# Branch A's norm factors: written to memory and read back into all partitions, instead of transposed by TensorE

## The chip, the core and the metric

The kernel runs on one core of one Trainium2 chip. The metric is the device time of one execution in microseconds (us). The core has five engines that run side by side, each through its own queue in order: TensorE (PE in the profile, with its weight loads as PEld), VectorE (DVE), ScalarE (ACT), GpSimd (POOL) and SyncE (SP), which here issues nearly all DMAs. TensorE writes to PSUM, which has eight banks of 128 x 512 float32. DVE and ACT read PSUM; POOL and the DMAs work on SBUF and on memory.

## What is computed

The program is one encoder block on 1024 tokens (and 16 meta tokens) of width 1024, all in float32. Cut to what matters here:

```
h = x + mixer(rms_norm(x));  h = h + swiglu(rms_norm(h));  out = rms_norm(h)

mixer:  y_a = differential_attention(q, k, v)       # branch A: 4 heads, v of width 128, all keys
        y_b = windowed_gqa(q, k, v, sink)           # branch B: 8 heads, window 128
        merged = sigmoid(ga) * (y_a @ w_ba) + sigmoid(gb) * (y_b @ w_bb)
        return merged @ w_o

differential_attention, at its end, for each token and head:
        y = y * rsqrt(mean(y * y over the 128 values) + 1e-6) * subln_gain * (1 - lambda_init)
```

The change is in that last line: one factor per token and head, `rsqrt(mean(y*y) + eps)`, has to reach the 128 values of that token.

## The kernel before

**Stages.** First x is normed and transposed, the projections are made, and branch B's attention runs (to about 306 us in the profile). Branch A's q, k and v go to memory by head (`qa_d`, `ka_d`, `va_d`). Then comes branch A's attention, to about 621 us: four heads h, each over eight tiles t of 128 query tokens, with the projection of the gates (`pp_g`, line 201) laid between its steps as filler for TensorE. After it come the branch outputs and gates (`ppa`, line 552), the product with w_o, and the feed-forward block, whose products are split into seven half-sized ones.

**One tile of branch A.** `scores_a` (from line 595 on) makes the scores of two maps, m = 1 and then m = 0, each in three chunks of keys (line 608, 352, 352 and 336 columns). DVE takes each chunk out of PSUM, adds the distance term and keeps the running minimum (line 614); ACT takes the exponent (619), DVE the reciprocal of the sum (620); POOL scales one map (622) and DVE combines the two (625). One tile later `transpose_a` turns the result by TensorE (637), with ACT and DVE splitting it into a high and a low part (640, 641). `values_a` multiplies by v (650) in three parts, for two tiles together. Its result has the 128 values of the head in the partitions and the tokens along the row: `py`, 128 x 512 for four tiles.

**The norm.** After every fourth tile `normed_a` (from 654 on) works on such a 128 x 512 block, which is called a chunk here: eight in all, c = 0 and 1 for each head. ACT squares it into `ysq` and scales a copy `yg` by the gain. Four matmuls sum the squares over the partitions: `ysq`'s 128 columns are the stationary operand and a column of ones is the moving one (663), so that token 128 i + p has its sum in partition p, column i of `pst`. DVE takes the mean (665), and POOL raises it to the power -1/2 (666) into `f`, 128 x 4. Three steps later four transposes (671) of a column of `f`, repeated 128 times, put the factor of each token in all 128 partitions of the PSUM bank `pf`; DVE multiplies `yg` by it (672), and SP stores the block to `ya_d` (673).

**The order.** TensorE's order is written out by hand. For each tile the string `SLOTS` (`SLOTS_LAST` in the last head) names the steps: s is the next score chunk, g is one step of a gate projection (three matmuls of 512 columns), t a group of transposes, and n a step of the tail. The tail is a list of generators, `values_a` followed, after every fourth tile, by `normed_a`; each n runs the first generator to its next `yield`, and a `for` loop of `N_WAIT` = 3 yields keeps the transposes of `f` away from their sums. At the start of a head ten g steps run in one piece. The other engines' orders and SP's order of DMAs are made by a scheduler when the program is built. The scores, the transposes, `pst` and `pf` share five PSUM banks (tag "sc"); a sixth one waits for the first to be read. q and k have one buffer for each map, so that the next head's loads (584 to 587) wait for the last scores of this head.

The functions that the diff touches, and those that call them:

Of the kernel before, what the change touches and what calls it, by code (L numbers as in the profile page):

```python
# [9 lines left out]
F32 = mybir.dt.float32  # L10
# [4 lines left out]
ALU = mybir.AluOpType  # L15
# [4 lines left out]
P = 128  # L20
# [7 lines left out]
AH = 4  # L28
# [5 lines left out]
LAMBDA_INIT = 0.2  # L34
FAR = 1e32
SC = 5
N_WAIT = 3
PP2 = 2
COMBINE_POOL = (0, 1, 2, 3)
SLOTS = "sgsgsngsgsgstntnt"  # L40
# [31 lines left out]
def encoder_block(ctx: ExitStack, tc: tile.TileContext, x, meta, norm_mix, w_in, lq1, lk1, lq2, lk2,  # L72
                  subln, sink, w_ba, w_bb, w_o, norm_ffn, w_g, w_u, w_d, norm_final, out, dbg=None):
    nc = tc.nc
# [8 lines left out]
    def pool(name, side="left", space=None, bufs=1):  # L83
        kw = {} if space is None else {"space": space}
        if space is not DRAM:
            kw["reuse_waits"] = "tile"
        cm = tc.tile_pool(name=name, bufs=bufs, side=side, **kw)
        p = cm.__enter__()
        return p, lambda: cm.__exit__(None, None, None)
# [3 lines left out]
    dram, close_dram = pool("dram", space=DRAM)  # L93

    def bank(p, tag, name, bufs):
        return p.tile([P, 512], F32, tag=tag, name=name, bufs=bufs)
# [3 lines left out]
    va_d = [dram.tile([P, 2, 9, P], F32, name=f"va_d{h}") for h in range(AH)]  # L100
    g_d = [dram.tile([P, S], F32, name=f"g_d{i}") for i in range(16)]
    ya_d = [dram.tile([P, S], F32, name=f"ya_d{h}") for h in range(4)]
    yb_d = [dram.tile([P, S], F32, name=f"yb_d{h}") for h in range(4)]

    ident = const.tile([P, P], F32, name="ident")
    make_identity(nc, ident)
    ones = const.tile([P, 1], F32, name="ones")
# [45 lines left out]
    psum2 = None  # L153
# [416 lines left out]
    apool, close_apool = pool("apool")  # L570
    psum2, close_psum2 = pool("psum2", space=PSUM)
# [82 lines left out]
    def normed_a(h, c, py):  # L654
        nm = f"{h}_{c}"
        ysq = apool.tile([P, 512], F32, tag="ysq", name=f"ysq_{nm}", bufs=1)
        nc.scalar.activation(ysq, py, AF.Square)
        yg = apool.tile([P, 512], F32, tag="yg", name=f"yg_{nm}", bufs=2)
        nc.scalar.activation(yg, py, AF.Copy, scale=gsub)
        yield  # L660
        pst = bank(psum2, "sc", f"apst_{nm}", SC)
        for i in range(4):
            nc.tensor.matmul(pst[:, i:i + 1], ysq[:, i * P:(i + 1) * P], ones, start=True, stop=True)
        f = small.tile([P, 4], F32, tag="af", name=f"af_{nm}", bufs=2)
        nc.vector.tensor_scalar(f, pst[:, 0:4], 1.0 / P, EPS, ALU.mult, ALU.add)
        nc.gpsimd.tensor_tensor(f, f, neg_half, ALU.pow)
        for _ in range(N_WAIT):
            yield
        pf = bank(psum2, "sc", f"apf_{nm}", SC)
        for i in range(4):  # L670
            nc.tensor.transpose(pf[:, i * P:(i + 1) * P], f[:, i:i + 1].broadcast_to([P, P]), ident)
        nc.vector.tensor_tensor(yg, yg, pf, ALU.mult)
        nc.sync.dma_start(ya_d[h][:, c * 512:c * 512 + 512], yg)
        yield

# [16 lines left out]
    def later(done):  # L692
        h, t, s, at_, v = done
        if t % 4 == 1:
            acc[0] = bank(psum2, "acc", f"apy_{h}_{t}", 1)
        yield from values_a(h, t, v, at_, acc[0])
        if t % 4 == 3:
            yield from normed_a(h, t // 4, acc[0])
# [9 lines left out]
    for n in range(AH * NT + T_LAG):  # L708
        scoring, turning = iter(()), iter(())
        if n < AH * NT:  # L710
            h, t = divmod(n, NT)
# [661 lines left out]
    for n in range(nf, len(steps)):  # L1373
        p, j = steps[n][1]
# [6 lines left out]
        if p in LOADS:  # L1381
            at, half, col = LOADS[p]
            if at <= j < at + 4:
                t, cols = 4 * half + j - at, slice(col * 512, col * 512 + 512)
# [63 lines left out]
```

## Time and profile before

| | |
|---|---|
| three timed runs | 1450.67, 1455.43 and 1457.50 us; median 1455.43 us |
| the profiled execution | 1448.28 us, of which the span of the profile is 1446.4 us |
| TensorE matmuls | 1429.9 us busy, 99% of the span |
| TensorE weight loads | 1228.3 us, 85% |
| DVE, ACT, POOL | 893.4 us (62%), 676.4 us (47%), 462.3 us (32%) |
| granted TensorE clock, mean | 0.997 of full speed |
| memory | 129.14 MB read, 53.94 MB written |
| the 32 transposes of `f` | 272 ns each, from 383.3 to 621.7 us |
| the 64 weight loads of `ysq` | 192 ns each, from 376.0 to 614.9 us |

A row of the timeline has the start and the length in us, the engine, the line, the operation, what it writes <- what it reads, and how many stand together. Matmuls are pipelined: the next one starts before the last one's record ends, so that the cost of one is the distance between starts, not the length of the record. A matmul of two float32 operands that are not rounded has two weight loads and two matmuls in the trace; so the 32 sums appear 64 times.

### The profile page before, as it was taken

How to read it: one execution, taken by the hardware profiler on the slowest of the kernel's cores; microseconds unless marked ns; L12 is line 12 of the kernel's file. 1: busy time of each engine (PE TensorE's matmuls, PEld its weight loads, DVE VectorE, ACT ScalarE, POOL GpSimd, SP SyncE). 2: the span in 40 equal slices, each digit the busy share in tenths (PEclk: the TensorE clock that was granted, in tenths of full speed). 3: DMA queues.
4: the chain of work that ended last, by engine and by line, in shares of the span. 5: the costliest groups of instructions: out<-in, count | busy, mean ns of one | idle time of the engine just before them, and what ended most of it. 6: DMA issues, size and time to landing. Idle time of an engine off the chain costs nothing.

```text
span 1446.4 us, 20973 instructions
## 1 busy us (share of the span) xinstructions
PE 1429.9 (99%) x7327; PEld 1228.3 (85%) x7327; DVE 893.4 (62%) x1756; ACT 676.4 (47%) x1275; POOL 462.3 (32%) x454
## 2 busy tenths in 40 slices
PE   8999999999999999999999999999999999999998
PEld 7998989888898989888878778888888888888886
DVE  6456326528787868545787955654455543787566
ACT  6356436535554545555345844333333333444444
POOL 4143223323332222221513035454444442000442
PEclk9999999999999999999999999999999999999999
DMA  7334443363424242077341633433223322964343
GB/s 239 88 102 114 112 126 100 77 200 106 144 84 147 74 147 75 30 263 246 103 166 73 182 109 110 138 131 103 102 95 109 102 100 96 343 206 141 126 124 146
DMA packets 158617, 191.01 MB, mean 132 GB/s; under 512 B 16096, under 2 KB 103584, under 8 KB 158512
## 3 DMA queue, kind: packets, MB, share of 16 engines
q1 hardware_dynamic: 157936, 188.63, 40.8%
q8 instruction: 58, 0.95, 0.3%
q10 hardware_dynamic: 576, 1.05, 0.2%
q14 instruction: 47, 0.39, 0.1%
HBM read 129.14 MB, written 53.94 MB: 127 GB/s over the span
## 4 chain that ended last, share of the span: by engine, by line
PE 89%; DMA 4%; DVE 3%; ACT 1%; issue 1%; POOL 1%; SPq 0%; ACTq 0%; DVEq 0%
PE pg L1219 27%; PE pd L1315 14%; PE pp_g L201 12%; PE aps L608 4%; PE po L1122 4%; PE apy L650 3%; PE pp_va L201 3%; PE pp_ka L201 3%; PE pp_qb L201 3%; PE pp_qa L201 3%; PE apt L637 2%; PE bpt L339 2%; PE bpy L345 2%; PE po L1130 2%; PE bps L314 2%
## 5 line engine op out<-in xcount | busy, mean ns | idle before, releaser
L1219 PE MATMUL pg<-t,wop 128*128 128x512 f32 x1056 | 242.4, 389 | 0.0
L1219 PEld LDWEIGHTS pg<-t,wop 128*128 128x128 f32 x1056 | 198.2, 188 | 41.2
L1315 PE MATMUL pd<-ob,oa 128*128 128x512 f32 x924 | 209.6, 389 | 0.0
L1315 PEld LDWEIGHTS pd<-ob,oa 128*128 128x128 f32 x924 | 173.4, 188 | 36.0
L114 POOL TENSOR_TENSOR wop<-wf,wop 128x512 fp32r<-128x512 f32 x114 | 149.4, 1311 | 166.6 <-ACT wop L113 156.7
L1219 PE MATMUL pg<-b,wop 128*128 128x512 f32 x792 | 184.2, 390 | 2.1 <-DVE c L1236 1.9
L1219 PEld LDWEIGHTS pg<-b,wop 128*128 128x128 f32 x792 | 148.2, 188 | 34.2 <-DVE c L1236 2.8
L114 POOL TENSOR_TENSOR wl_c<-w_c,wh_c 128x1024 fp32r<-128x1024 f32 x32 | 77.6, 2426 | 162.1 <-ACT wh_c L113 142.5
L113 ACT ACTIVATE wop<-wf 128x512 fp32r<-128x512 f32 x128 | 80.8, 633 | 80.9 <-PE pg L1219 53.3
L619 ACT ACTIVATE as<-as,amn 128x1040 f32<-128x1040 f32 x64 | 74.5, 1164 | 73.8 <-DVE amn L614 73.6
L201 PE MATMUL pp_g<-hT_hi,wh_c 128*128 128x512 f32 x256 | 101.3, 396 | 0.0
L201 PE MATMUL pp_g<-hT_hi,wl_c 128*128 128x512 f32 x256 | 100.9, 394 | 0.0
L201 PE MATMUL pp_g<-hT_lo,wh_c 128*128 128x512 f32 x256 | 100.9, 394 | 0.0
L113 ACT ACTIVATE oa<-ra 128x512 fp32r<-128x512 f32 x77 | 48.7, 632 | 107.5 <-PE pd L1315 48.9
L608 PE MATMUL aps<-ak,aq 128*128 128x352 f32 (+1 forms) x384 | 92.6, 326 | 0.0
L114 POOL TENSOR_TENSOR oa<-ra,oa 128x512 fp32r<-128x512 f32 x27 | 34.9, 1294 | 168.6 <-ACT oa L113 167.2
L991 DVE TENSOR_TENSOR s<-wf,wf 128x512 f32<-128x512 f32 x22 | 16.0, 727 | 117.3 <-DMA wf<-in_w_ff_up_dram 70.0
L608 PEld LDWEIGHTS aps<-ak,aq 128*128 128x128 f32 x384 | 69.6, 188 | 14.0
L614 DVE CUSTOM_DVE_ANT_0 as<-aps,dist,amn 128x352 f32<-128x352 f32 (+1 forms) x128 | 71.3, 564 | 10.2 <-PE aps L608 8.1
L326 POOL TENSOR_SCALAR bs<-bs,bdn 128x432 f32<-128x432 f32 (+1 forms) x64 | 37.0, 596 | 87.1 <-DVE bdn L324 64.7
L614 DVE CUSTOM_DVE_ANT_0 as<-aps,dist,far_a 128x352 f32<-128x352 f32 x64 | 37.1, 580 | 43.0 <-PE aps L608 42.7
L316 DVE CUSTOM_DVE_ANT_0 bs<-bps,tbx,nsink 128x432 f32<-128x432 f32 (+1 forms) x64 | 38.4, 625 | 40.8 <-PE bps L314 37.7
(274 smaller groups left out, 3043.5 us busy)
## 6 DMA issues: line engine op xcount, KB each, us to landing
ra<-aop SPq DMA_DIRECT2D x77, 256.0 KB, 2.6
w_c<-in_w_in_dram SPq DMA_DIRECT2D x33, 512.0 KB, 4.0
wf<-in_w_ff_gate_dram SPq DMA_DIRECT2D x25, 512.0 KB, 3.6
wf<-in_w_ff_up_dram SPq DMA_DIRECT2D x25, 512.0 KB, 3.6
aop<-as SPq DMA_DIRECT2D x44, 256.0 KB, 2.0
aop<-c SPq DMA_DIRECT2D x33, 256.0 KB, 2.0
g_d<-gate_stage SPq DMA_DIRECT2D x32, 256.0 KB, 2.0
gt<-g_d SPq DMA_DIRECT2D x32, 256.0 KB, 3.8
```

The costliest lines, as they stand in the source:

```text
L113: nc.scalar.activation(hi, src, AF.Copy)
L114: lo_eng.tensor_tensor(lo, src, f32(hi), ALU.subtract)
L201: nc.tensor.matmul(ps[:, :n], a[:, c, :], b[:, c, at:at + n], start=(c == 0 and i == 0), stop=(c == DC - 1 and i == 2))
L316: nc.vector.tensor_tensor_reduce(st[:, r, :W], ps[:, :W], tb, 2.0 ** -(4 * g + r + 1), nsink[:, 4 * g + r:4 * g + r + 1], ALU.add, ALU.min ...
L326: nc.gpsimd.tensor_scalar(st[:, r, :W], st[:, r, :W], dn[:, r:r + 1], 1.0, ALU.mult, ALU.mult)
L608: nc.tensor.matmul(ps[:, :n], qs[m][:, t * P:(t + 1) * P], ks[m][:, vv, k0:k0 + n], start=(vv == 0), stop=(vv == 1))
L614: nc.vector.tensor_tensor_reduce(s[m][:, a:b], ps[:, a - k0:b - k0], far_by, slope, low, ALU.add, ALU.min, mn[:, m, i + j:i + j + 1])
L619: nc.scalar.activation(s[m][:, 0:L], s[m][:, 0:L], AF.Exp, bias=low, scale=-1.0, accum_out=dn[:, m:m + 1])
L650: nc.tensor.matmul(py[:, cols], v[:kp, a, k, :], at_[:kp, k, b, :], start=(k == 0 and j == 0), stop=(k == 8))
L1122: nc.tensor.matmul(sets_o[p][u], oa[:, a, u * P:(u + 1) * P], ob[:, b, :], start=(p in (1, 5) and j == 0 and k == 0), stop=(p in (2, 3) an ...
L1219: nc.tensor.matmul(ps, op[:, x, c, :], b[:, y, c, :], start=(p in (1, 5) and c == 0 and n == 0), stop=(p in (4, 2, 3) and c == 3 and n == ...
L1315: nc.tensor.matmul(ps[u], oa[:, a, u * P:(u + 1) * P], ob[:, b, :], start=(p in (1, 2, 5) and j == 0 and k == 0), stop=(p in (2, 3, 4) and ...
```

## The change

The factors of a chunk go through memory. The sums are taken in another order of tokens: `ysq` is read as a stationary operand with a step of four elements, so that partition p of `pst` and of `f` holds the four neighbouring tokens 4 p to 4 p + 3. `f` (128 x 4) is then stored to a small tensor in memory, `f_d`, where it lies as one row of 512 factors in the tokens' order, and a second DMA reads that row into all 128 partitions of `fb`, which takes the buffer of `ysq`. DVE multiplies `yg` by `fb`. The transposes, their PSUM bank and the three empty yields are gone; `normed_a` has two yields in place of five, so that what stands behind it in the tail comes up to three n steps earlier.

```diff
-N_WAIT = 3
...
+    f_d = [dram.tile([P, 4], F32, name=f"f_d{i}") for i in range(2 * AH)]
...
         pst = bank(psum2, "sc", f"apst_{nm}", SC)
         for i in range(4):
-            nc.tensor.matmul(pst[:, i:i + 1], ysq[:, i * P:(i + 1) * P], ones, start=True, stop=True)
+            nc.tensor.matmul(pst[:, i:i + 1], ysq.rearrange("p (t i) -> p i t", i=4)[:, i, :], ones, start=True, stop=True)
+
         f = small.tile([P, 4], F32, tag="af", name=f"af_{nm}", bufs=2)
         nc.vector.tensor_scalar(f, pst[:, 0:4], 1.0 / P, EPS, ALU.mult, ALU.add)
         nc.gpsimd.tensor_tensor(f, f, neg_half, ALU.pow)
-        for _ in range(N_WAIT):
-            yield
-        pf = bank(psum2, "sc", f"apf_{nm}", SC)
-        for i in range(4):
-            nc.tensor.transpose(pf[:, i * P:(i + 1) * P], f[:, i:i + 1].broadcast_to([P, P]), ident)
-        nc.vector.tensor_tensor(yg, yg, pf, ALU.mult)
+        nc.sync.dma_start(f_d[2 * h + c], f)
+        fb = apool.tile([P, 512], F32, tag="ysq", name=f"fb_{nm}", bufs=1)
+        nc.sync.dma_start(fb, f_d[2 * h + c].rearrange("(o p) i -> o (p i)", o=1).broadcast_to([P, 512]))
+        nc.vector.tensor_tensor(yg, yg, fb, ALU.mult)
         nc.sync.dma_start(ya_d[h][:, c * 512:c * 512 + 512], yg)
         yield
```

## The prediction, made before the changed kernel ran

> **What bounds the kernel now.** I read the page first (span, busy shares, granted clock, chain), then the list of what TensorE waited for, then the same engine by stretches of time.
>
> ```profile
> span 1446.4 us, 20973 instructions
> ...
> PE 1429.9 (99%) x7327; PEld 1228.3 (85%) x7327; DVE 893.4 (62%) x1756; ACT 676.4 (47%) x1275; POOL 462.3 (32%) x454
> ...
> PEclk9999999999999999999999999999999999999999
> ...
> PE 89%; DMA 4%; DVE 3%; ACT 1%; issue 1%; POOL 1%; SPq 0%; ACTq 0%; DVEq 0%
> ```
>
> TensorE is busy for 99% of the span at its full granted clock, and it is 89% of the chain that ended last. Its waits over the whole execution are nine groups, in order of size; these are the first and the last:
>
> ```profile
> PE po L1122 <- DVE gt L900: 2.4, 1, 2.4
> ...
> PE pg L1219 <- ACT c L1231: 0.2, 1, 0.2
> ```
>
> None of the nine is in branch A's attention, where the change lies. Busy time by stretches says the same of that stage (PE, then PEld, DVE, ACT, POOL):
>
> ```profile
> 500.00:600.00 100.00, 100.00 (x628) 91.14 (x627) 79.42 (x267) 54.68 (x101) 29.77 (x32) 1.00 0.28 88
> ```
>
> So there, time taken from TensorE's queue is time won, and everything else costs only what it makes TensorE wait. DVE is next, at 79%.
>
> **The change, part by part.** *The transposes go.* Eight groups of four leave TensorE's queue.
>
> ```profile
> 382.86 0.60 PE L637 MATMUL apt<-ident,as 128*128 128x128 f32 x4
> 383.30 0.60 PE L671 MATMUL apf<-ident,af 128*128 128x128 f32 x4
> 383.73 0.60 PE L637 MATMUL apt<-ident,as 128*128 128x128 f32 x4
> ```
>
> From the start of the group to the start of the next are 383.73 - 383.30 = 0.43 us; eight groups are **-3.4 us**. The other record of the same instructions reads larger:
>
> ```profile
> L671 PE MATMUL apf<-ident,af x32: 272/272/273, 383.3 to 621.7; 128*128 128x128 f32 x32
> ```
>
> 32 x 272 ns would be 8.7 us, but the starts above are 0.11 us apart, since the records overlap. The Trainium skill (TensorE: Matmul & The Clock Gate, Part 4: PE-mode transpose) gives about 275 ns for a transpose inside a kernel; taken as the price of each, that would make the sum -8.8 us, past half a per cent faster. The record's length agrees with it, the spacing does not support it as a price, and a stage in which TensorE is always busy pays by spacing.
>
> *The sums read `ysq` with a step of four.* The same 32 matmuls (64 in the trace) stay, but their stationary operand is no longer contiguous.
>
> ```profile
> 376.10 0.95 PE L663 MATMUL apst<-ones,ysq 128*128 128x1 f32 x8
> 376.91 0.74 PE L637 MATMUL apt<-ident,as 128*128 128x128 f32 x5
> ```
>
> ```profile
> L663 PEld LDWEIGHTS apst<-ones,ysq x64: 187/192/192, 376.0 to 614.9; 128*128 128x128 f32 x64
> ```
>
> ```profile
> L671 PEld LDWEIGHTS apf<-ident,af x32: 133/137/138, 383.2 to 621.6; 128*128 128x128 f32 x32
> ```
>
> ```profile
> L637 PEld LDWEIGHTS apt<-ident,as 128*128 128x128 f32 x288 | 34.5, 142 | 1.1 <-issue 0.4 <-DVE as L625 0.2
> ```
>
> With one moving column, a group is paced by its loads: eight in 376.91 - 376.10 = 0.81 us. No load with a step of four is in the trace. The lower end is nothing: the one load that isn't contiguous (a column repeated, 137 ns) is no slower than the contiguous one of the same kind (142 ns). A gain is excluded, because the loads stay as many. The upper end is twice the time, 8 x 0.81 = +6.5 us. I take 0, the row that is nearest, and keep 6.5 for a rival.
>
> *The factor's way through memory.* For each chunk come two more DMAs on SP, and DVE's multiply waits for the second. The order of the built program shows that multiply, for six of the eight chunks, among the DVE steps of a later tile's scores, before work that TensorE waits for; in the first chunk it stands after line 625, in the last at the end of the stage. I follow chunk (1,1), head 1, second half:
>
> ```profile
> L666 POOL TENSOR_TENSOR af<-af,neg_half x1: 1040/1040/1040, 490.8 to 490.8; 128x4 f32<-128x4 f32 x1
> ```
>
> ```profile
> 489.68 0.40 SPq L172 DMA_DIRECT2D w_c<-in_w_in_dram  x1
> ```
>
> ```profile
> DMA to landing us min/median/max: 3.7/3.7/3.7
> ```
>
> ```profile
> ra<-aop SPq DMA_DIRECT2D x77, 256.0 KB, 2.6
> ...
> ak<-ka_d SPq DMA_DIRECT2D x8, 520.0 KB, 7.7
> ...
> aq<-qa_d SPq DMA_DIRECT2D x8, 512.0 KB, 5.7
> ...
> yb_d<-by SPq DMA_DIRECT2D x64, 32.0 KB, 1.9
> ...
> nfin<-in_norm_final_dram SPq DMA_DIRECT2D x1, 512.0 KB, 4.1
> ```
>
> ```profile
> 494.50 0.57 DVE L614 CUSTOM_DVE_ANT_0 as<-aps,dist,amn 128x352 f32<-128x352 f32 x1
> ...
> 495.22 0.23 DVE L614 CUSTOM_DVE_ANT_0 as<-aps,no_dist,amn 128x16 f32<-128x16 f32 x1
> ```
>
> `f` is ready at 490.8 + 1.04 = 491.8; the weights ahead of it in the queue land at 489.7 + 3.7 = 493.4. The store is the size of no row; as the smallest store shown (1.9 us) it lands at about 493.8, and SP, which waits for that, issues the load then. The load is 128 rows of 2 KB out of one: 2.6 us as the quick load of 256 KB, 4.1 us as the broadcast of 512 KB. So `fb` lands at 496.4 to 497.9. DVE comes to its multiply between the two rows above, at 495.2, plus the nine `py` matmuls that the shorter tail now sets ahead of these scores (1.15 us by the next fence): 496.3. It waits 0.1 to 1.6 us, and behind it stand the last score chunk, the reciprocals and the transposes' low parts. What that may cost is the slack of the PSUM banks:
>
> ```profile
> 367.06 0.47 PE L608 MATMUL aps<-ak,aq 128*128 128x336 f32 x2
> ...
> 367.73 1.31 PE L650 MATMUL apy<-at,av 128*128 128x256 f32 x9
> 368.88 0.60 PE L637 MATMUL apt<-ident,as 128*128 128x128 f32 x4
> ...
> 371.28 0.49 PE L608 MATMUL aps<-ak,aq 128*128 128x352 f32 x2
> ```
>
> ```profile
> 367.85 0.55 DVE L614 CUSTOM_DVE_ANT_0 as<-aps,dist,amn 128x320 f32<-128x320 f32 x1
> ```
>
> The last chunk's bank is filled at 367.06, read until 367.85 + 0.55 = 368.4, and wanted again five banks later (three groups of transposes, a score chunk, the next) at 371.28: 2.9 us of slack. A wait of 1.6 us hides in it, so I take 0. The `py` matmuls only change places, and one PSUM bank less is asked for in each chunk.
>
> *What SP delays.* At a head's start the new DMAs stand among the next head's q and k loads.
>
> ```profile
> 380.03 0.32 SPq L584 DMA_DIRECT2D aq<-qa_d  x1
> ...
> 383.05 0.33 SPq L584 DMA_DIRECT2D aq<-qa_d  x1
> ...
> 383.90 1.10 SPq L587 DMA_DIRECT2D ak<-ka_d  x2
> ```
>
> ```profile
> DMA to landing us min/median/max: 10.6/10.7/10.8
> ```
>
> ```profile
> 396.41 0.48 PE L608 MATMUL aps<-ak,aq 128*128 128x352 f32 x2
> ```
>
> The last piece of k for m = 0 is issued at 384.4 and lands 10.8 us later, at 395.2; its first matmul starts at 396.41, 1.2 us after. Ahead of it now lie the 256 KB of `fb`: 0.8 us at the fastest slice of the page's GB/s row, 343, or 2.1 us if half of `nfin`'s broadcast takes half of its 4.1 us.
>
> ```profile
> GB/s 239 88 102 114 112 126 100 77 200 106 144 84 147 74 147 75 30 263 246 103 166 73 182 109 110 138 131 103 102 95 109 102 100 96 343 206 141 126 124 146
> ```
>
> Over the 1.2 us, at three head starts, that is 0 to 3 x 0.9 = 2.7 us. SP's wait for `f_d` (behind the 512 KB of `aq`, 5.7 us, so to 386 instead of 383.05) delays the issue, not the data, as a load that waits over 10 us stands in the queue. I take 0. If the queue were empty, those 3 us less the 1.2 would come on top: 1.8 at each of three starts, 5.4 us in all.
>
> *The seam behind the stage.* SP's order also differs among the first loads of the branch outputs.
>
> ```profile
> 634.79 0.40 PE L201 MATMUL pp_g<-hT_hi,wl_c 128*128 128x512 f32 x1
> 635.02 0.63 PE L552 MATMUL ppa<-yb,wbhb 128*128 128x512 f32 x2
> ```
>
> TensorE passes from gates to branch outputs without a gap, and the factors of the last chunk are made under 20 us of gates. I take 0, with the 2.4 us of the `po` wait as the size of what a changed order may cost or save.
>
> *Sum.* 1448.28 - 3.4 = 1444.9 us against the profiled execution. That execution lies 7.15 us below the median of the three timed runs, 1455.43; against the median I forecast 1455.43 - 3.4 = **1452.0 us**, -0.24%. A measurement of this kernel tells about 0.5% (7.3 us) from no change.
>
> **The rivals.** *Strided loads at half speed.* For: each of the 128 columns of a load now comes from another 16 bytes, and the group is paced by nothing but its loads (0.81 us for eight). Against: no row shows a load slowed by its pattern. Price +6.5, in sum 1455.43 - 3.4 + 6.5 = 1458.5 us. The Trainium skill (SBUF — State Buffer, Specifications) says that SBUF has lines of 16 bytes, that full rate needs at least two hits on a line, and that each crossing to a new line pays; by that rule the changed read, one hit on each line, is slow. A note further down on that page counts a step of up to four float32 as free, so the page alone does not decide, and no run here shows it yet.
>
> *DVE waits at its multiply for longer than the banks cover* (the other side: slower). For: DVE runs in order, at 79%, and the load shares a queue whose k loads take 7.7 us. Against: in chunk (1,1) nothing large is ahead. It decides once `fb` takes over 2.9 us more than DVE's arrival: 496.3 + 2.9 - 493.8 = 5.4 us from issue to landing. At 7.7 us TensorE loses 2.3 us in each of seven chunks, 16.1 us: 1455.43 - 3.4 + 16.1 = 1468.1 us.
>
> *The gain is given back behind the stage.* The seam's loads, in their new order, or the wait at `po` take up the 3.4 us: 1455.4 us. For: many of SP's places change there. Against: no gap at the seam, and DVE, ACT and SP get their work earlier, too. *The transposes cost their records' length* (8.7 us): 1446.7 us. Against it stands their spacing.
>
> **How the numbers follow.** Forecast 0.43, strided loads 0.32, DVE's wait 0.13, given back 0.10, transposes at 272 ns 0.02. The range starts at the forecast less the distance of the lowest timed run from the median (1455.43 - 1450.67 = 4.8), 1447, and ends at the strided rival with the loads at the head starts (2.7) and the scatter to the highest run (2.1), 1463.3; the DVE rival is left out. The forecast alone would be 1447 to 1455. Faster by over 0.5% needs 3.9 us more than the transposes hold by their spacing: 0.06, of which 0.02 for their full length and 0.04 for scatter. Slower by over 0.5% is DVE's wait, 0.13, and the upper part of the strided rival, 0.09: 0.22. Within 0.5%: 0.72.
>
> **What would show it.** No row of line 671's transposes; the start of a `pst` group to the next instruction 0.81 us (right) or about 1.6 us with longer PEld rows (strided rival); no TensorE wait on DVE in the stage, though DVE idles before its multiply on a DMA for up to 1.6 us; `fb` landing in 2.6 to 4.1 us; the first score of a head's m = 0 map not waiting for `ak`. The forecast is wrong if TensorE waits on DVE or on `ak` by more than 3 us in sum, or if `ppa` starts with a gap.

## The result and the profile after

The changed kernel takes 1468.32 us (median of 6 runs, 1463.21 to 1471.15), the kernel before 1452.24 us (6 runs, 1448.25 to 1457.5): ratio 1.0101, interval 1.0083 to 1.012. The change costs 1%, some 16 us; the forecast was 1452.0 us, within a range that ended at 1463.3. It was worked out from three runs of the kernel before with a median of 1455.43 us; of six the median is 1452.24, so where -3.4 us were forecast, +16 were measured. The profiled execution of the changed kernel took 1463.65 us, 15.4 more than that of before (1448.28).

The page of the changed kernel looks almost like that of before, here its span and busy shares.

```profile
span 1461.9 us, 20950 instructions
...
PE 1439.1 (98%) x7295; PEld 1234.3 (84%) x7295; DVE 894.0 (61%) x1756; ACT 677.5 (46%) x1275; POOL 464.5 (32%) x454
```

TensorE has 32 instructions fewer and is busy 9.2 us longer; of the 15.5 us that the span grew, 6.3 are idle time. A busy share of 98% for 99% tells no more than that. The stages tell where: the first sum of the factors (line 663), the first `ppa` and the first `po` of the changed kernel start here; the last two lines are the `po` of the kernel after and before.

```profile
376.43 1.92 PE L663 MATMUL apst<-ones,ysq 128*128 128x1 f32 x8
378.21 0.74 PE L637 MATMUL apt<-ident,as 128*128 128x128 f32 x5
```

```profile
645.78 11.08 PE L552 MATMUL ppa<-yb,wbhb 128*128 128x512 f32 x48
659.63 0.73 PE L552 MATMUL ppa<-yb,wbhb 128*128 128x512 f32 x2 [2.77 <-ACT wbhb L113]
660.98 34.09 PE L552 MATMUL ppa<-yb,wbhb 128*128 128x512 f32 x142 [0.62 <-POOL wbhb L114]
```

```profile
738.42 1.30 PE L1121 MATMUL po<-ob_o,oa_o 128*128 128x512 f32 x5
```

```profile
722.10 1.07 PE L1122 MATMUL po<-ob_o,oa_o 128*128 128x512 f32 x4
```

The first sum to the first `ppa` is called the attention stage below. It takes 645.78 - 376.43 = 269.35 us, before 635.02 - 376.10 = 258.92: **+10.4 us**. From there to `po`, the `ppa` stage, 738.42 - 645.78 = 92.64 us, before 722.10 - 635.02 = 87.08: **+5.6 us**. What lies ahead and behind differs by half a microsecond in sum.

In the attention stage two things are to be seen. The group of sums takes 378.21 - 376.43 = 1.78 us to the next instruction, where it took 0.81, and its loads are longer (192 ns before):

```profile
L663 PEld LDWEIGHTS apst<-ones,ysq x64: 308/330/332, 376.3 to 625.9; 128*128 128x128 f32 x64
```

And there are waits where there were none. These are all of TensorE's in that stretch, then DVE's waits at its multiply (total in us, times, longest). The view counts a wait only from the end of the record before it; from start to start these stops hold about 6 us.

```profile
PE aps L608 <- DMA ak<-ka_d: 1.4, 1, 1.4
PE apt L637 <- DVE amn L614: 1.2, 2, 1.1
PE apt L637 <- DVE as L625: 0.6, 1, 0.6
PE apy L650 <- DVE at L641: 0.3, 1, 0.3
```

```profile
DVE yg L671 <- DMA fb<-f_d: 20.0, 8, 6.6
```

DVE stands at its multiply in all eight chunks. The fifth one, (2,0), shows how that gets to TensorE. DVE and SP of the changed kernel, and SP of the kernel before at the same place:

```profile
533.79 0.69 DVE L671 TENSOR_TENSOR yg<-yg,fb 128x512 f32<-128x512 f32 x1 [3.62 <-DMA fb<-f_d]
534.40 0.58 DVE L614 CUSTOM_DVE_ANT_0 as<-aps,dist,far_a 128x352 f32<-128x352 f32 x1
```

```profile
526.78 0.32 SPq L668 DMA_DIRECT2D f_d<-af  x1
529.07 0.32 SPq L670 DMA_DIRECT2D fb<-f_d  x1
...
534.51 0.33 SPq L672 DMA_DIRECT2D ya_d<-yg  x1
534.89 0.50 SPq L584 DMA_DIRECT2D aq<-qa_d  x1
```

```profile
527.53 0.33 SPq L584 DMA_DIRECT2D aq<-qa_d  x1
...
530.23 0.33 SPq L673 DMA_DIRECT2D ya_d<-yg  x1
```

`fb` is issued 2.3 us after the store of `f`, and DVE's multiply starts 4.7 us later. DVE waits 3.62 us, more than the 2.9 us of slack of the prediction, and TensorE then waits 1.1 us for a score chunk to be read. SP waits too: the store of `yg` stands behind the multiply, and the next head's q and k stand behind the store, so they are issued at 534.9 instead of 527.5, which is the wait of 1.4 us for `ak` a little later.

At the seam the first `ppa` starts without a gap, as before, and 11 us later TensorE waits for the third weight. SP of the changed kernel, then of before:

```profile
647.45 0.38 SPq L856 DMA_DIRECT2D m<-in_w_out_dram  x1
647.92 1.62 SPq L821 DMA_DIRECT2D raw_ya<-ya_d  x3
...
651.20 3.03 SPq L544 DMA_DIRECT2D wbrb<-in_w_branch_b_dram  x3
```

```profile
638.47 0.98 SPq L544 DMA_DIRECT2D wbrb<-in_w_branch_b_dram  x2
639.55 0.45 SPq L857 DMA_DIRECT2D m<-in_w_out_dram  x1
```

The load of `w_o` (into `m`, line 856, before 857) stands ahead of the weight now and stood behind it; the weight is issued 651.20 - 645.78 = 5.4 us after the first `ppa`, before 638.47 - 635.02 = 3.45 us. SP has to wait 3.0 us before it can issue the load of `w_o`, with four loads of `ya` and the weight behind it:

```profile
SPq L856 <- DMA m<-yb_d: 1.6, 1, 1.6
SPq L856 <- DVE yb L114: 1.4, 1, 1.4
```

TensorE's wait is 2.77 + 0.62 = 3.4 us, and the stage lost 5.6. The granted clock of TensorE, the third column from the right, has most of the rest:

```profile
660.00:662.00 2.00, 1.38 (x6) 0.84 (x5) 2.00 (x3) 1.81 (x4) 2.00 (x2) 0.91 1.07 367
662.00:664.00 2.00, 2.00 (x6) 1.54 (x5) 1.77 (x2) 0.07 (x1) 2.00 (x2) 0.50 1.06 387
664.00:666.00 2.00, 2.00 (x8) 1.62 (x7) 0.79 (x2) 0.64 (x1) 1.56 (x2) 0.74 1.05 386
```

After the wait the clock is halved for some 3.4 us: 2 x (0.09 + 0.50 + 0.26) = 1.7 us more. A slice of the page is 36.5 us wide and shows a 9 there.

### The profile page after: what moved, and what is told of

The parts are those of the page before. It is cut to its first block, busy times and chain, and to the rows that moved or that the text cites. A ratio compares the mean times of both kernels' runs of the same rounds, so it can differ in the third digit from the quotient of the medians.

```text
span 1461.9 us, 20950 instructions
## 1 busy us (share of the span) xinstructions
PE 1439.1 (98%) x7295; PEld 1234.3 (84%) x7295; DVE 894.0 (61%) x1756; ACT 677.5 (46%) x1275; POOL 464.5 (32%) x454
## 4 chain that ended last, share of the span: by engine, by line
PE 86%; DMA 6%; DVE 4%; issue 1%; ACT 1%; POOL 1%; SPq 0%; DVEq 0%; POOLq 0%; ACTq 0%
PE pg L1218 27%; PE pd L1314 14%; PE pp_g L201 8%; PE ppa L552 4%; PE po L1121 4%; PE aps L608 3%; PE pp_qb L201 3%; PE pp_va L201 3%; PE pp_ka L201 3%; PE pp_qa L201 3%; PE apy L650 3%; PE bpt L339 2%; PE apt L637 2%; PE bpy L345 2%; PE po L1129 2%; PE bps L314 1%
## 5 line engine op out<-in xcount | busy, mean ns | idle before, releaser
L990 DVE TENSOR_TENSOR s<-wf,wf 128x512 f32<-128x512 f32 x22 | 15.5, 705 | 117.6 <-DMA wf<-in_w_ff_up_dram 70.7
L614 DVE CUSTOM_DVE_ANT_0 as<-aps,dist,amn 128x320 f32<-128x320 f32 (+1 forms) x128 | 71.3, 563 | 9.7 <-PE aps L608 7.9
L622 POOL TENSOR_SCALAR as<-as,adn,neglam 128x1040 f32<-128x1040 f32 x32 | 38.9, 1215 | 78.8 <-DVE adn L620 78.8
```

What stands on the lines that cost most here:

```text
L614: nc.vector.tensor_tensor_reduce(s[m][:, a:b], ps[:, a - k0:b - k0], far_by, slope, low, ALU.add, ALU.min, mn[:, m, i + j:i + j + 1])
L622: (nc.gpsimd if t % 4 in COMBINE_POOL else nc.vector).tensor_scalar(s[1][:, 0:L], s[1][:, 0:L], dn[:, 1:2], neglam, ALU.mult, ALU.mult)
```

## The experiments

The theory after the traces has four causes (the strided loads, DVE's and SP's waits for the factor's way through memory, the shorter tail in TensorE's order, the order at the seam) against the gain of the transposes. The rivals are in the expectation of each run. The kernel before was timed beside the runs, with medians of 1451.5 to 1453.2 us, and the ratios are against these. Stage lengths are from each run's own profile, start to start, as above. They leave out what happens elsewhere: in the profiles of s1, t1, c1, f1 and q5 TensorE waits 1.6 to 2.2 us in the very first tile of the attention, ahead of the first sum, where the edits change no work. But each is of one execution, and some hold time at half the granted clock, as seen at the seam: 3.4 us in the attention stage of d1 and 1.7 us each in those of c1, d2 and p1.

| run | us (median) | ratio to before, interval | attention stage | ppa stage |
|---|---|---|---|---|
| before | 1452.24 | 1 | 258.92 | 87.08 |
| after | 1468.32 | 1.0101 (1.0083 to 1.012) | 269.35 | 92.64 |
| s1_strided | 1459.51 | 1.0044 (1.003 to 1.0058) | 266.32 | 87.08 |
| c1_contiguous | 1467.16 | 1.0101 (1.0084 to 1.0117) | 269.04 | 92.21 |
| t1_no_transposes | 1449.3 | 0.9973 (0.9961 to 0.9984) | 255.51 | 87.08 |
| f1_seam_fixed | 1461.58 | 1.0063 (1.0045 to 1.0082) | 270.18 | 87.17 |
| c2_contiguous_by_act | 1464.51 | 1.0087 (1.0066 to 1.0109) | 267.36 | 94.96 |
| q2_pool_queue | 1456.67 | 1.0037 (1.0023 to 1.0051) | 264.76 | 87.81 |
| q3_pool_queue_contiguous | 1452.91 | 1.0007 (0.9991 to 1.0023) | 260.35 | 87.93 |
| d1_memory_only | 1460.41 | 1.0055 (1.0034 to 1.0076) | 271.32 | 87.08 |
| d2_memory_only_pool | 1455.6 | 1.0028 (1.0014 to 1.0042) | 262.66 | 88.27 |
| d3_small_load | 1453.88 | 1.001 (0.9997 to 1.0023) | 260.38 | 87.14 |
| p1_pool_multiplies | 1468.56 | 1.0124 (1.0106 to 1.0142) | 270.45 | 94.58 |
| b1_sums_in_one_pass | 1454.88 | 1.0034 (1.0017 to 1.0051) | 258.55 | 87.08 |
| v1_short_tail | 1448.67 | 0.9968 (0.9954 to 0.9982) | 256.05 | 87.08 |
| y1_store_from_pool | 1469.12 | 1.0108 (1.0089 to 1.0127) | 269.54 | 94.90 |
| q4_pool_queue_tail | 1457.95 | 1.0028 (1.0015 to 1.0041) | 263.40 | 87.75 |
| q5_pool_queue_tail_contiguous | 1453.64 | 0.9999 (0.9979 to 1.0019) | 258.33 | 88.70 |

**s1: the strided loads alone.** Kernel before, with

```diff
-            nc.tensor.matmul(pst[:, i:i + 1], ysq[:, i * P:(i + 1) * P], ones, start=True, stop=True)
+            nc.tensor.matmul(pst[:, i:i + 1], ysq.rearrange("p (t i) -> p i t", i=4)[:, i, :], ones, start=True, stop=True)
...
-        nc.vector.tensor_tensor(yg, yg, pf, ALU.mult)
+        nc.vector.tensor_tensor(yg.rearrange("p (t i) -> p t i", i=4), yg.rearrange("p (t i) -> p t i", i=4),
+                                pf.rearrange("p (i t) -> p t i", i=4), ALU.mult)
```

> The kernel before, with its transposes and its waits, but the sums read ysq with a step of four (DVE puts the factors back in order as it reads them from PSUM). The steps on the other engines keep their order. Theory (four causes: strided loads, DVE's wait for fb, the k loads behind it, the seam): the loads of line 663 take about 330 ns instead of 192, a group of eight about 1.78 us instead of 0.81, so +7.7 us and nothing else: about 1460 us beside 1452 of before, attention stage of branch A (first sum to first ppa) about 266.5 us instead of 259. Rival (the loads were slow in the changed kernel only because the traffic of the new DMAs got in their way): 192 ns, 0.81 us, the time of before.

The loads of this run, with no new DMA anywhere near them:

```profile
L663 PEld LDWEIGHTS apst<-ones,ysq x64: 307/330/332, 380.6 to 626.7; 128*128 128x128 f32 x64
```

The stage grew by 266.32 - 258.92 = 7.40 us, as expected to a few tenths; the `ppa` stage did not move. The strided read costs this by itself, and traffic has no part in it.

**c1: the changed kernel with contiguous loads.**

```diff
-            nc.tensor.matmul(pst[:, i:i + 1], ysq.rearrange("p (t i) -> p i t", i=4)[:, i, :], ones, start=True, stop=True)
+            nc.tensor.matmul(pst[:, i:i + 1], ysq[:, i * P:(i + 1) * P], ones, start=True, stop=True)
...
-        nc.vector.tensor_tensor(yg, yg, fb, ALU.mult)
+        nc.vector.tensor_tensor(yg.rearrange("p (i t) -> p i t", i=4), yg.rearrange("p (i t) -> p i t", i=4),
+                                fb.rearrange("p (t i) -> p i t", i=4), ALU.mult)
```

> The changed kernel, with the sums reading ysq contiguously; DVE reads fb with a step of four instead, so that the result is the same. Theory: the loads are back at 192 ns, -7.7 us against the changed kernel, about 1460.5 us; the waits for fb (PE on DVE and on ak, some 5 us) and the seam (some 5 us) stay. Rival (traffic slows the loads): they stay at 330 ns and the time stays at 1468.

The loads went back to 192 ns, and the stage became 0.3 us shorter: a miss for the theory, though not in favour of the rival. Two rows on DVE tell what was given back, its multiply (693 ns in the changed kernel) and its wait (20.0 us there):

```profile
L671 DVE TENSOR_TENSOR yg<-yg,fb x8: 1062/1072/1096, 393.9 to 635.5; 128x512 f32<-128x512 f32 x8
...
  DMA fb<-f_d: 25.4, 8
```

The step of four had moved to DVE's operand and costs 0.38 us there in each chunk, 3.0 us of DVE in all; and DVE waits 5.4 us longer. Which of the two undid the gain this run cannot tell; c2 can.

**t1: the transposes alone.** Kernel before, with the transposes left out:

```diff
-        pf = bank(psum2, "sc", f"apf_{nm}", SC)
-        for i in range(4):
-            nc.tensor.transpose(pf[:, i * P:(i + 1) * P], f[:, i:i + 1].broadcast_to([P, P]), ident)
-        nc.vector.tensor_tensor(yg, yg, pf, ALU.mult)
+        nc.vector.tensor_tensor(yg, yg, ysq, ALU.mult)
```

> The kernel before without the transposes of line 671 and without the factors in the output: yg is multiplied by ysq instead of by pf. No DMA is added and no load is strided, but the built order puts the high copies of ob_o1 ahead of that of wbhb_2 on ScalarE at the seam, as in the changed kernel. Theory: the attention stage gets 3.4 us shorter (259.1 to about 255.7), and the ppa stage 3 to 6 us longer (87.2 to 90 to 93) from the order alone, with a TensorE wait for wbhb on ACT: 1451 to 1455 us in all. Rival (the seam's loss comes from the last chunk's way through memory): ppa stays 87.2 us and the time falls to about 1448.8.

The stage is 258.92 - 255.51 = 3.41 us shorter: the transposes are worth what their spacing said. At the seam the theory missed: with the same order on ScalarE and SP as in the changed kernel, all 192 matmuls of branch B run through without a gap,

```profile
634.96 43.72 PE L552 MATMUL ppa<-yb,wbhb 128*128 128x512 f32 x192
```

So the changed order alone costs nothing. Here the load of `w_o` is issued at 626.68, 8.3 us ahead of the first `ppa`, and the weight 637.44 - 634.96 = 2.5 us after it; probably all this is early because the last chunk's multiply waits for nothing.

**f1: the seam alone.** The changed kernel, with two more weights loaded ahead of the loop:

```diff
+    first_w += [branch_w(ypool, o, w_bb, "b") for o in (2, 3)]
...
-        w = first_w[o] if o < 2 else branch_w(ypool, o, w_bb, "b")
+        w = first_w[o] if o < 4 else branch_w(ypool, o, w_bb, "b")
```

> The changed kernel, but the weights wbrb_2 and wbrb_3 are loaded and split ahead of the loop, as those of 0 and 1 are, so that no high copy of ob_o1 stands ahead of wbhb_2 on ScalarE. Everything of branch A's attention stays as changed. Theory: no wait of TensorE for wbhb, ppa stage back from 92.8 to about 87.2 us, -5.5 us: about 1463 us. Rival (the last chunk's loads make the seam late): the wait stays and the time is about 1468.

```profile
650.24 43.81 PE L552 MATMUL ppa<-yb,wbhb 128*128 128x512 f32 x192
```

No gap is left, the stage is 92.64 - 87.17 = 5.47 us shorter, and the time 1461.58 us. On SP the third weight now stands ahead of the loads of `ya` (though still behind `w_o`) and is issued 653.45 - 650.24 = 3.2 us after the first `ppa`; on ScalarE it is copied ahead of `ob_o`, behind which it stood. So the order at the seam decides it, where `w_o` is held up. The run moves both engines and does not tell them apart; in the changed kernel the weight had landed 0.9 us before ScalarE copied it (658.05 and 658.96), so SP's part of the 3.4 us is the larger.

**c2: contiguous loads, without the slow multiply.** The changed kernel with contiguous loads, with ScalarE bringing the squares into their order:

```diff
-        nc.scalar.activation(ysq, py, AF.Square)
+        nc.scalar.activation(ysq.rearrange("p (i t) -> p i t", i=4), py.rearrange("p (t i) -> p i t", i=4), AF.Square)
```

> The changed kernel; ScalarE squares py into ysq in the order in which the loads want it (it reads PSUM with a step of four), so that the sums load contiguously, and DVE's multiply reads fb as in the changed kernel. No other instruction changes. Loads 192 ns. Theory A (the causes add up; the run before gained nothing only because its multiply took 1.07 us instead of 0.69): the stage gets 7.5 us shorter, 269.35 to about 262, 1461 us in all. Theory B (the causes share one wait: DVE stands at its multiply until fb lands, and what TensorE saves ahead of it is waited there): DVE's idle time for fb grows from 20 us to some 25, TensorE's waits for DVE grow, the stage gains 4 us at most, 1464 us or more.

DVE's multiply takes 691 ns again, and waits:

```profile
  DMA fb<-f_d: 26.3, 8
```

The stage gained 269.35 - 267.36 = 1.99 us of the 7.40 that the loads cost in s1, DVE's wait grew by 6.3 us, and TensorE's waits for DVE in the stage grew from 2.1 to 6.7 us: theory B. Behind the sums TensorE and DVE run until DVE stands at its multiply, and time saved ahead of that is waited there. It also answers c1: the 1.7 us by which c1's stage is longer than c2's are time at half clock (0.78, 0.50 and 0.87 granted in the three stretches of 2 us from 614 us on, behind a wait of 2.0 us), so the slower multiply cost TensorE next to nothing, and the waits undid the gain.

**q2: the store of `f` and the load of `fb` on GpSimd's queue.**

```diff
-        nc.sync.dma_start(f_d[2 * h + c], f)
+        nc.gpsimd.dma_start(f_d[2 * h + c], f)
...
-        nc.sync.dma_start(fb, f_d[2 * h + c].rearrange("(o p) i -> o (p i)", o=1).broadcast_to([P, 512]))
+        nc.gpsimd.dma_start(fb, f_d[2 * h + c].rearrange("(o p) i -> o (p i)", o=1).broadcast_to([P, 512]))
```

> The changed kernel, with the store of f and the load of fb issued by GpSimd instead of SP. The loads stay strided. In the built order DVE's multiply now stands 23 to 29 DVE instructions behind the reading of the sums instead of 13 to 26, and the loads at the seam are in the order of before. Theory (loss beyond the strided loads = DVE's and SP's waits for fb and the seam): no wait of TensorE for DVE's multiply or for ak, ppa stage 87.1 us, stage 258.9 - 3.4 + 7.5 = 263 us; in all 1452.25 - 3.4 + 7.5 = 1456.4 us. Rival (the way through memory costs in itself, whatever the queue and the place of the multiply): 1465 us or more.

TensorE's waits in the whole stage are now:

```profile
PE apy L650 <- DVE at L641: 0.3, 1, 0.3
PE apy L650 <- ACT at L640: 0.2, 1, 0.2
```

The stage is 269.35 - 264.76 = 4.59 us shorter, the `ppa` stage 4.83; 1456.67 us, as expected. So here the way through memory isn't dear in itself; SP's queue, the place of the multiply, or both made it so. The run changes both, and does not tell them apart.

**q3: the same with contiguous loads** (the diffs of q2 and c2 together).

> As the run with GpSimd's queue, and with ScalarE writing the squares in the order of the loads, so that these are contiguous. Theory: only the transposes' gain is left, 1452.25 - 3.4 = 1448.9 us, stage 255.5 us, ppa stage 87.1 us. Theory B of the run with contiguous loads on SP's queue says the same here, since no wait is left to share; if this run stays above 1453 us, another cost was missed.

The stage is 4.9 us longer than expected: 260.35 instead of 255.5. DVE's wait for `fb`, 18.2 us in q2, is 24.8 us here, and TensorE waits for DVE again (1.0 us in two waits for `amn`). Theory B is not confined to SP's queue: with the quick loads DVE stands longer before `fb` lands here as well.

**d1, d2, d3: the transfers alone.** The kernel before, with its transposes, and with

```diff
+        nc.sync.dma_start(f_d[2 * h + c], f)
+        fb = apool.tile([P, 512], F32, tag="ysq", name=f"fb_{nm}", bufs=1)
+        nc.sync.dma_start(fb, f_d[2 * h + c].rearrange("(o p) i -> o (p i)", o=1).broadcast_to([P, 512]))
         for _ in range(N_WAIT):
```

> The kernel before with its transposes, its contiguous loads and its waits; the store of f and the load of fb are issued on SP as well, but nothing reads fb, so that DVE never waits for it. Only SP's order differs from before. Theory: the transfers themselves are hidden, 1452 us as before, with at most 1.5 us for loads of k that stand behind them; rival (traffic, or SP standing still until f_d has landed, is the cost): a TensorE wait for ak at the head starts, and up to 5.4 us more.

```profile
PE aps L609 <- DMA ak<-ka_d: 7.9, 5, 2.6
```

The stage is 12.4 us longer, more than in the changed kernel, though nothing reads `fb`: a miss for the theory. (By the medians the whole run is 1460.41 - 1451.95 = 8.5 us longer.) 7.9 us are waits for k; and the two longest of them go over into half the clock, of which these are the rows of the first:

```profile
472.00:474.00 2.00, 0.49 (x2) 0.19 (x1) 0.00 (x0) 0.63 (x2) 0.00 (x0) 1.00 1.08 288
474.00:476.00 2.00, 0.89 (x3) 0.82 (x4) 0.21 (x1) 0.00 (x0) 0.00 (x0) 0.72 0.32 91
476.00:478.00 2.00, 2.00 (x7) 1.72 (x6) 0.80 (x4) 0.00 (x0) 1.21 (x1) 0.50 0.01 4
```

The next two runs ask what of the transfers does it: in d2 both are issued by GpSimd (`nc.gpsimd.dma_start`), in d3 SP brings back only `f` (`nc.sync.dma_start(fb[:, 0:4], f_d[2 * h + c])`).

> As the run with the transfers alone (kernel before, store of f and load of fb added, nothing reads fb), but GpSimd issues both, so that SP never stands still for f_d. The bytes are the same. Theory (SP's standing still until f_d has landed, which issues the loads of k late, is most of the loss): 1452 to 1454 us, TensorE waits for ak under 1.5 us in sum. Rival (the traffic of fb itself, 256 KB read out of one row of 2 KB, holds up the loads of k): 1457 us or more, waits for ak as in the run with SP's queue (7.9 us).

> As the run with the transfers alone on SP, but the load brings back only the 2 KB of f (128 rows of 16 bytes) instead of the 256 KB of fb. SP's order is the same, and it waits for f_d as there. Theory (standing still): 1457 us or more, waits for ak stay over 5 us. Rival (traffic): 1452 to 1454 us, waits for ak under 1.5 us.

TensorE's waits for k, in d2 and in d3:

```profile
PE aps L609 <- DMA ak<-ka_d: 1.8, 1, 1.8
```

```profile
PE aps L609 <- DMA ak<-ka_d: 1.2, 1, 1.2
```

Neither theory holds. The bytes without SP's standing still cost 3.7 us in the stage (262.66), the standing still without the bytes 1.5 us (260.38), both together 12.4 us. In d2 1.8 of the 3.7 us are the wait and 1.7 the half clock behind it. The waits alone, 1.8 and 1.2 us against 7.9, do not add up either. One explanation would be that the two delays add up in front of the same loads, which by the prediction's count landed only 1.2 us before their use, so that all beyond that is paid; no run shows this.

**p1 and y1: DVE's wait alone, SP's wait alone.** In the changed kernel, p1 has `nc.gpsimd.tensor_tensor(yg, yg, fb, ALU.mult)`, so that DVE does not wait for `fb`; y1 has `nc.gpsimd.dma_start(ya_d[h][:, c * 512:c * 512 + 512], yg)`, so that SP doesn't wait for the multiply.

> The changed kernel (strided loads, SP's queue), with the multiply by fb on GpSimd instead of DVE, so that DVE never stands still for fb. TensorE's order is the same. Theory (DVE's wait costs TensorE 3 to 4 us): no row of DVE waiting for fb, stage 269.35 to about 265.5 us; 1464.5 us in all if the seam stays as in the changed kernel. Rival (the wait only moves: GpSimd's scaling of the scores stands behind its multiply, and DVE and TensorE behind that): stage 268 us or more, with TensorE waiting for DVE's line 625.

> The changed kernel, with the store of yg (ya_d) issued by GpSimd instead of SP, so that SP does not stand still for DVE's multiply with the loads of k behind it. f and fb stay on SP, and DVE's multiply stands at the same place among DVE's instructions. Theory (DVE's wait for fb holds up TensorE both by DVE itself and by the loads of k behind ya_d): the wait for ak at head 3 goes, the waits for DVE (1.2 us before the transposes at about 534 and after) stay: stage 269.35 to about 267.5 us. Rival (all of it comes by SP): stage 264.8 us, as with GpSimd's queue.

The first waits of TensorE in the stage, in p1 and in y1:

```profile
PE aps L608 <- DMA ak<-ka_d: 2.5, 2, 1.8
PE aps L608 <- DVE amn L614: 0.5, 1, 0.5
PE apt L637 <- POOL as L626: 0.4, 1, 0.4
```

```profile
PE apt L637 <- DVE amn L614: 1.8, 2, 1.6
PE aps L608 <- DMA ak<-ka_d: 0.7, 1, 0.7
```

Neither gained: 270.45 and 269.54 us beside 269.35, and p1's stage would still be 268.7 without the 1.7 us of half clock behind its wait of 1.8 us. Without DVE's wait the wait for k grows from 1.4 to 2.5 us; without SP's, TensorE's waits for DVE's line 614 grow from 1.2 to 1.8. Theory and rival both miss in y1; in p1 the rival's length came true, by the loads of k rather than by line 625.

**v1 and q4: the shorter tail.** v1 is t1 without the three yields; q4 is q2 with three yields ahead of the multiply.

> The run without transposes (contiguous loads, no memory, factors left out of the output), and without the three yields as well, so that the py matmuls of the next pair come earlier in TensorE's order, as in the changed kernel. Beside the run without transposes it shows what the shorter tail does alone. Theory: the small waits at the end of the stage that all kernels without the yields show (0.35, 0.38, 0.39 and 0.61 us) are the tail's: stage 255.5 + 1.7 = 257.2 us. Rival (they belong to the wait for fb): stage 255.5 us.

> The run with GpSimd's queue (strided loads), and with three yields put back ahead of the multiply, so that TensorE's order is that of the kernel before without its transposes. Theory: the tail's 1.7 us go, stage 264.76 to about 263 us (258.92 - 3.41 + 7.5); in all about 1455 us. Rival: stage stays at 264.8 us.

Without the tail's three steps the stage is 256.05 - 255.51 = 0.54 us longer in v1; with them put back it is 264.76 - 263.40 = 1.36 us shorter in q4. So by the stages the shorter tail costs 0.5 to 1.4 us, less than expected in v1; the totals are too coarse to confirm it, as the intervals of t1 and v1, and those of q2 and q4, overlap. q4, with 263.40, is 0.5 us from 258.92 - 3.41 + 7.40 = 262.91.

**q5: everything undone but the transposes.** q4 with contiguous loads (the diff of c2).

> GpSimd's queue, the three yields, and squares written by ScalarE in the order of the loads, so that these are contiguous: all four costs that the runs showed are taken away, and the gain of the transposes should be left. Theory: stage 255.5 to 257 us, ppa stage 87.1 us, 1449 to 1450.5 us, just ahead of both kernels. Rival (with fast loads DVE catches up with fb again, as in the run with GpSimd's queue and contiguous loads): stage 259 us or more, 1452 us or more.

```profile
PE aps L608 <- DMA ak<-ka_d: 1.5, 2, 0.9
PE apt L637 <- DVE as L625: 0.6, 1, 0.6
```

```profile
DVE yg L673 <- DMA fb<-f_d: 27.2, 8, 8.3
```

1453.64 us beside 1453.18 of before, ratio 0.9999 (0.9979 to 1.0019): no gain. The attention stage keeps 0.6 of the 3.4 us; TensorE waits 1.5 us for k and 0.6 for DVE, which stands at its multiply for 27.2 us.

**b1: another way to shorten the sums.** The kernel before, with squares and ones in fp32r, one pass for each sum:

```diff
-        ysq = apool.tile([P, 512], F32, tag="ysq", name=f"ysq_{nm}", bufs=1)
+        ysq = apool.tile([P, 512], F32R, tag="ysq", name=f"ysq_{nm}", bufs=1)
...
-            nc.tensor.matmul(pst[:, i:i + 1], ysq[:, i * P:(i + 1) * P], ones, start=True, stop=True)
+            nc.tensor.matmul(pst[:, 2 * i:2 * i + 2], ysq[:, i * P:(i + 1) * P], ones_r, start=True, stop=True)
...
```

> The kernel before, with the squares and the ones of the sums rounded to fp32r, so that each sum is one load and one matmul (of two columns) instead of two passes: four loads for a chunk instead of eight. Theory (a group of sums is paced by its loads): 4 x 0.11 = 0.4 us less in each of eight groups, -3.2 us: about 1449 us, as much as the transposes' removal was worth. Rival (the time saved is waited elsewhere, since DVE is close behind): 1451 to 1452 us.

The loads are halved in number, and the stage gained 0.4 of 3.2 us; TensorE waits 2.3 us in two waits for ScalarE's line 621. That is the rival's side for the stage. The total is above both: in the profiled run 5.3 us more are lost in the last stages, where nothing is edited and TensorE's matmuls come some 1% slower for 400 us at a full granted clock; that was not followed up.

Of the versions with the whole computation none ran ahead of the kernel before; t1 and v1 leave the factors out.

## Why the prediction was wrong

- **The transposes**, -3.4 us by the spacing of their starts. Right: -3.41 us in t1. The 272 ns of their records would have been 8.7.
- **The strided loads**, 0, "the row that is nearest". This is the first step that failed. The row was a load of one column 128 times over, which reads a single address; it was near in form, and says nothing about 128 addresses 16 bytes apart. The rival for the strided loads had the mechanism, but its price of twice the time, 6.5 us, was itself a guess; the measured spacing is 0.97 us a group more, 7.40 us for the stage in s1. The Trainium skill (SBUF — State Buffer, Specifications) asks for two hits on each line of 16 bytes for full rate; the trace agrees, 330 ns with one hit beside 192 with four. The note on SBUF lines further down on that page of the Trainium skill, by which four float32 are a free step, does not hold here: neither for these loads nor for DVE's read in c1, 1.07 us beside 0.69.
- **DVE's wait**, 0, since the 1.6 us in chunk (1,1) hide in 2.9 us of slack. In that chunk it was right (DVE waited 1.16 us). The failing step is that one chunk stood for eight. The text had seen that at the head starts the loads of k lie in the same queue, and had treated that as a cost for k alone; but there `fb` is late as well, and DVE waited 3.3, 1.7 and 3.6 us in chunks (0,0), (1,0) and (2,0).
- **SP's delays**, 0, with the words that the wait for `f_d` "delays the issue, not the data". The runs showed the opposite: d1's stage lost 12.4 us by the transfers alone, and neither the bytes nor the standing still could be priced by itself (3.7 and 1.5 us). What the text did not follow at all is that the store of `yg`, which waits for the multiply, stands ahead of the next head's q and k.
- **The tail**, 0: 0.5 to 1.4 us.
- **The seam**, 0, with 2.4 us for either side: 5.6 us. That TensorE passed this place without a gap was a fact about the old order and the old times of SP's loads, and the prediction knew that the order had changed. By t1 the new order alone is harmless; the gap comes where `w_o`, now ahead, holds up the queue for 3.0 us. It looked for a gap at the first `ppa`, where the weights are loaded long before; the third weight is the one that moved.

In one order of taking the causes away, the sum closes: -3.41 (t1), +7.40 (s1), +4.59 (SP's queue and the place of the multiply: the changed kernel less q2), +1.36 (tail: q2 less q4), and 0.49 that no run explains, give the 10.43 us of the attention stage; 5.47 of the 5.56 us at the seam are f1's. In another order the terms are others: with the waits in place the strided loads cost 1.99 us (c2), without them 4.4 (q2 less q3) to 7.40 (s1).

The rival "DVE waits at its multiply" named 1468.1 us, and 1468.32 was measured. That is chance: it priced seven stalls of 2.3 us, and TensorE's waits for DVE in the stage are 2.1 us in all. What stays open is the split of the 4.59 us between DVE and SP, since p1 and y1, which take away one each, both gain nothing.

## What to carry to other kernels

An operation taken from the engine that sets the time was worth its spacing here, not its record, as long as nothing that replaced it stood in a queue ahead of that engine's next input. The round trip through memory put three things there: the bytes, the issuing engine's wait for the store, and whatever was queued behind the reader. Follow the new DMAs at the place where the queue is fullest, not at a quiet one, and where the order of loads changes look at each load's distance to its use, not at the gap that isn't there yet. Where two engines run close, a saving on one is first paid into the other's wait, so price an edit in the kernel in which it will stand.

## What the hardware showed that was not expected

- A stall of TensorE can cost more than its length. Waits of 2.77 us (seam of the changed kernel), 2.6 us (twice in d1), 2.0 us (late in c1's attention stage) and 1.8 us (p1 and d2) each brought some 3.4 us at half the granted clock, 1.7 us more. The wait of 1.4 us for `ak` in the changed kernel, the one of 2.4 us at `po` in the kernel before and even one of 3.1 us at `po` in v1 did not. The Trainium skill (TensorE: Matmul & The Clock Gate, Part 1) describes this gate, half rate after an idle window of about 3.4 us; the half rate and the length agree, but here stalls shorter than a window were enough.
- The clock records of the 18 traces show which. In each trace the changes of the clock lie on one grid of 3.41 us (in the changed kernel 641.71 us, 188 steps, pass between two half-clock stretches), and a step with over about half of its time idle is followed by one at half clock. From 40 us to the last few us the clock was halved 24 times. 23 times TensorE was idle for 1.82 to 3.41 us of the step ahead, once for 1.53, and no step with more than 1.82 us went without. The 3.1 us in v1 fell into two steps, 1.75 and 1.34 us. So whether a wait of 2 us costs another 1.7 is the luck of where it falls.
- The scatter of one kernel goes with this clock. Of 97 executions of the kernel before, those at a granted clock of 0.998 took 1449.2 us in the mean (16 of them) and those at 0.994 1455.1 (14), 5.9 us more; 0.4% of 1450 us are 5.8.
- A step of four float32 slows reads of SBUF, for TensorE's loads (192 to 330 ns, and 0.11 to 0.23 us apart) and for DVE (0.69 to 1.07 us), but steps in reads of PSUM cost DVE and ScalarE nothing here. The rows are DVE's multiply in s1, which reads PSUM with a step of 128 float32, and ScalarE's square in c2, with a step of four; with contiguous reads they took 687 ns (kernel before) and 598 ns (changed kernel):

```profile
L672 DVE TENSOR_TENSOR yg<-yg,apf x8: 681/686/690, 389.7 to 634.1; 128x512 f32<-128x512 f32 x8
```

```profile
L657 ACT ACTIVATE ysq<-apy x8: 582/598/603, 371.4 to 620.2; 128x512 f32<-128x512 f32 x8
```
